# A small store of zeros early on ACT, and the last slab stored whole, in a FiLM layer kernel

## The chip, the cores and the metric

The kernel runs on one core of a Trainium2 chip. The metric is device time in microseconds (us) of one execution; lower is better. Executions of this kernel mostly agree within a few tenths of a microsecond. Some are longer: where one is over 1.5% above the fastest of the same kernel it is marked slow. A ratio is the mean time of one kernel's fast runs over the mean of the other's fast runs of the same rounds, so it is not quite the ratio of the medians that I quote.

## The reference

```python
batch, seq, dim, cond_dim = 32, 512, 256, 64          # all float32
gamma = conditioning @ gamma_proj                     # [32, 256]
beta  = conditioning @ beta_proj
return x * (1 + gamma[:, None, :]) + beta[:, None, :] # [32, 512, 256]
```

16.8 MB of x come in and 16.8 MB go out. Nothing else is large.

## The kernel before

x is cut into four slabs of eight batches. A slab is 128 partitions x 32 rows of 256 numbers, 4 MB. All four fit in SBUF at once, so no load ever waits for a buffer. SyncE issues the loads, ACT issues the small loads and all stores. DVE works on 11 rows of each group of 16 and GpSimd (POOL) on 5, and each group is stored when both are done.

```python
cond_s = consts.tile([batch, cond_dim], f32)
nc.scalar.dma_start(out=cond_s, in_=conditioning)
gbproj = consts.tile([cond_dim, 2 * dim], f32)
nc.scalar.dma_start(out=gbproj[:, :dim], in_=gamma_proj)
nc.scalar.dma_start(out=gbproj[:, dim:], in_=beta_proj)

for s in range(SLABS):                       # 5 loads: 8 + 24 rows, then 32, 32, 32
    ...
        nc.sync.dma_start(out=xs[:, r : r + n, :], in_=x_v[s, :, r : r + n, :])
# ... identity, matmuls: gamma and beta per partition in PSUM (gb_p) and SBUF (gb_s)
for s in range(SLABS):
    ...
    for r0 in range(0, ROWS, GROUP):         # two groups of 16 rows
        nc.vector.scalar_tensor_tensor(out=v, in0=rows(g_p, nv), scalar=1.0, in1=v, ...)
        nc.gpsimd.tensor_tensor(out=w, in0=w, in1=rows(g_s, nw), op=ALU.mult)
        nc.vector.tensor_add(out=v, in0=v, in1=rows(b_p, nv))
        nc.gpsimd.tensor_tensor(out=w, in0=w, in1=rows(b_s, nw), op=ALU.add)
        nc.scalar.dma_start(out=o_v[s, :, r0 : r0 + GROUP, :],
                            in_=xs[:, r0 : r0 + GROUP, :])
```

## Time and profile before

| | before |
|---|---|
| time, median of 6 runs | 84.43 us (84.36 to 84.56) |
| profiled span (length of the one run that the profile shows) | 82.6 us |
| DMA queues, share of 16 engines' time | 48.6% + 48.0% |
| DVE / POOL busy | 49.9 / 46.2 us |
| first load packet, last store packet | 1.74 us, 81.38 us |

Read it as one resource that never rests. Sixteen DMA engines serve two queues, q1 (loads, issued on SyncE) and q10 (all that ACT issues). A packet here is one row of a transfer on one engine: 8, 24 or 32 KB per partition for the loads, 16 KB for the stores, 1 KB for gamma and beta, 4 bytes for a semaphore, the counter by which a finished transfer releases what waits for it. Below, a queue's ring is the line of its packets that wait for one engine, and a turn is what an engine takes from one ring before it goes over to the other. DVE and POOL are busy for 60% and 56% of the span and idle at its end.

### The profile page before, as it was taken

The numbers are of one execution on the slowest core, as the hardware profiler recorded it, in microseconds if no ns is written. First come the engines' busy times: TensorE is split into PE (matmuls) and PEld (weight loads), VectorE is DVE, ScalarE is ACT, GpSimd is POOL, SyncE is SP. The second block draws the span as 40 slices with busy tenths as digits, with TensorE's granted clock in tenths as the row PEclk, the third lists the DMA queues.
The fourth block names the chain that finished last, engine by engine and source line by source line (L and its number), as shares of the span: only waits on it lengthen the run. The fifth ranks groups of instructions, "written<-read, shape, count | busy, mean of one in ns | idle before, by whom it ended". The sixth has DMA issues, their size and how long they took to land.

```text
span 82.6 us, 156 instructions
## 1 busy us (share of the span) xinstructions
PE 9.1 (11%) x10; PEld 2.8 (3%) x10; DVE 49.9 (60%) x18; ACT 3.9 (5%) x9; POOL 46.2 (56%) x22
## 2 busy tenths in 40 slices
PE   0080000899600000000000000000000000000000
PEld 0100000443000000000000000000000000000000
DVE  2011000059999999999999999999999920000000
ACT  0600000034400000000000000000000000000000
POOL 2000000069999999999999999999995000000000
DMA  3899999969969989998889979899999999999992
GB/s 56 337 508 397 389 397 524 460 302 508 508 270 492 508 381 381 413 476 381 381 381 556 460 302 460 381 468 421 429 452 389 468 421 421 460 389 452 437 421 87
DMA packets 2080, 33.69 MB, mean 408 GB/s; under 512 B 288, under 2 KB 416, under 8 KB 416
## 3 DMA queue, kind: packets, MB, share of 16 engines
q1 hardware_dynamic: 720, 16.78, 48.6%
q10 hardware_dynamic: 1360, 16.92, 48.0%
HBM read 16.92 MB, written 16.78 MB: 408 GB/s over the span
## 4 chain that ended last, share of the span: by engine, by line
DVE 49%; DMA 16%; issue 11%; PE 2%; ACTq 1%; ACT 1%
DVE xs L100 30%; DVE xs L103 19%; DMA gbproj<-in_beta_proj_dram 16%; PE gb_p L79 2%; ACTq L50 1%; ACTq L48 0%; ACT gb_s L82 0%; ACT gb_s L85 0%
## 5 line engine op out<-in xcount | busy, mean ns | idle before, releaser
L102 POOL TENSOR_TENSOR xs<-xs,gb_s 128x1280 f32<-128x1280 f32 x8 | 23.0, 2895 | 16.2 <-ACT gb_s L82 16.2
L100 DVE SCALAR_TENSOR_TENSOR xs<-gb_p,xs 128x2816 f32<-128x2816 f32 x8 | 24.7, 3083 | 10.9 <-ACT gb_s L85 10.9
L103 DVE TENSOR_TENSOR xs<-xs,gb_p 128x2816 f32<-128x2816 f32 x8 | 24.7, 3086 | 0.3
L104 POOL TENSOR_TENSOR xs<-xs,gb_s 128x1280 f32<-128x1280 f32 x8 | 23.0, 2893 | 0.0
L79 PE MATMUL gb_p<-gbproj,cond_T 64*128 64x512 f32 x8 | 7.2, 1074 | 8.9 <-DMA gbproj<-in_beta_proj_dram 8.9
L74 DVE COPY cond_T<-cond_T_p 64x512 f32<-64x512 f32 x1 | 0.7, 683 | 4.3 <-PE cond_T_p L72 4.3
L79 PEld LDWEIGHTS gb_p<-gbproj,cond_T 64*128 64x128 f32 x8 | 2.5, 328 | 13.7 <-issue 13.7
L72 PE MATMUL cond_T_p<-rident,cond_s 32*64 32x512 f32 x2 | 1.9, 1065 | 3.9 <-DMA cond_s<-in_conditioning_dram 3.9
L82 ACT ACTIVATE gb_s<-gb_p 128x256 f32<-128x256 f32 x4 | 1.5, 383 | 16.4 <-PE gb_p L79 16.4
L85 ACT COPY gb_s<-gb_p 128x256 f32<-128x256 f32 x4 | 1.5, 367 | 0.0
L82 ACT ACT_TABLE_LOAD x1 | 1.3, 1283 | 2.4 <-issue 2.4
L67 DVE COPY rident<-ident 32x512 f32<-32x512 f32 x1 | 0.4, 416 | 1.2 <-POOL ident masks.py:199 1.2
L72 PEld LDWEIGHTS cond_T_p<-rident,cond_s 32*64 32x64 f32 x2 | 0.3, 202 | 3.9 <-issue 3.9
masks.py:197 POOL MEMSET ident<- 32x32 f32 x1 | 0.1, 114 | 0.3 <-POOLq L121 0.3
masks.py:199 POOL TENSOR_SCALAR_AFFINE_SELECT ident<-ident 32x32 f32<-32x32 f32 x1 | 0.2, 202 | 0.1
L121 POOL MEMSET const-float32-0.0<- 128x1 f32 x1 | 0.1, 103 | 0.2 <-issue 0.2
L121 POOL MEMSET const-bfloat16-1.0<- 128x1 bf16 x1 | 0.1, 106 | 0.0
L121 POOL MEMSET const-uint8-127<- 128x1 uint8 x1 | 0.1, 106 | 0.0
L121 POOL MEMSET const-float32-1.0<- 128x1 f32 x1 | 0.1, 103 | 0.0
## 6 DMA issues: line engine op xcount, KB each, us to landing
out_dram<-xs ACTq DMA_DIRECT2D x8, 2048.0 KB, 18.2
xs<-in_x_dram SPq DMA_DIRECT2D x3, 4096.0 KB, 32.9
xs<-in_x_dram SPq DMA_DIRECT2D x1, 3072.0 KB, 12.2
xs<-in_x_dram SPq DMA_DIRECT2D x1, 1024.0 KB, 4.6
gbproj<-in_gamma_proj_dram ACTq DMA_DIRECT2D x1, 64.0 KB, 9.1
gbproj<-in_beta_proj_dram ACTq DMA_DIRECT2D x1, 64.0 KB, 12.9
cond_s<-in_conditioning_dram ACTq DMA_DIRECT2D x1, 8.0 KB, 3.0
```

The lines of the kernel that those rows point to most:

```text
L50: nc.scalar.dma_start(out=gbproj[:, :dim], in_=gamma_proj)
L67: nc.vector.tensor_copy(out=rident.rearrange("p (b g) -> p b g", g=REP), in_=ident.to_broadcast([batch, batch, REP]),)
L72: nc.tensor.matmul(cond_T_p, lhsT=cond_s, rhs=rident, start=True, stop=True)
L74: nc.vector.tensor_copy(out=cond_T, in_=cond_T_p)
L79: nc.tensor.matmul(p_t, lhsT=cond_T[:, s * P : (s + 1) * P], rhs=gbproj, start=True, stop=True)
L82: nc.scalar.activation(out=s_t[:, :dim], in_=p_t[:, :dim], func=mybir.ActivationFunctionType.Identity, bias=1.0, scale=1.0)
L85: nc.scalar.copy(out=s_t[:, dim:], in_=p_t[:, dim:])
L100: nc.vector.scalar_tensor_tensor(out=v, in0=rows(g_p, nv), scalar=1.0, in1=v, op0=ALU.add, op1=ALU.mult)
L102: nc.gpsimd.tensor_tensor(out=w, in0=w, in1=rows(g_s, nw), op=ALU.mult)
L103: nc.vector.tensor_add(out=v, in0=v, in1=rows(b_p, nv))
L104: nc.gpsimd.tensor_tensor(out=w, in0=w, in1=rows(b_s, nw), op=ALU.add)
L121: nc = _bacc.Bacc("TRN2", target_bir_lowering=False, num_devices=1)
```

## The change

A store of 16 rows of zeros (16 KB) into the output is added. The zeros are issued on ACT, ahead of gamma and beta; their place in the output is overwritten later by the first real store. The last slab goes out in one 4 MB store in place of two of 2 MB. The number of DMAs stays at sixteen. What the zeros were meant to achieve isn't stated; the form suggests an attempt to reorder what is in flight around the small loads and to save one DMA at the end.

```diff
     nc.scalar.dma_start(out=cond_s, in_=conditioning)
+
+    zero = consts.tile([16, dim], f32)
+    nc.gpsimd.memset(zero, 0.0)
+    nc.scalar.dma_start(out=o_v[0, 0:16, 0, :], in_=zero)
     gbproj = consts.tile([cond_dim, 2 * dim], f32)
...
+            last = s == SLABS - 1
...
-            nc.scalar.dma_start(out=o_v[s, :, r0 : r0 + GROUP, :],
-                                in_=xs[:, r0 : r0 + GROUP, :])
+            e0 = 0 if last else r0
+            if not last or r0 + GROUP == ROWS:
+                nc.scalar.dma_start(out=o_v[s, :, e0 : r0 + GROUP, :],
+                                    in_=xs[:, e0 : r0 + GROUP, :])
```

## The prediction

> **What bounds the kernel now.** I read the page's slices and queues first, then the chain of waits in order of time, then the stretches of the end, then the source line of the stores, and last the single packet records of the DMA engines in the trace.
>
> ```profile
> PE   0080000899600000000000000000000000000000
> DVE  2011000059999999999999999999999920000000
> POOL 2000000069999999999999999999995000000000
> DMA  3899999969969989998889979899999999999992
> q1 hardware_dynamic: 720, 16.78, 48.6%
> q10 hardware_dynamic: 1360, 16.92, 48.0%
> ```
>
> The DMA row is full from the second slice to the last but one, while DVE and POOL are idle for the last fifth. q1 holds the loads issued on SyncE, q10 everything issued on ACT. Together their packets fill 96.6% of the time of 16 engines: 0.966 x 82.57 us = 79.8 us by the page. I counted it from the packet records too: 128 load packets of 8 KB at 0.309 us, 128 of 24 KB at 0.92, 384 of 32 KB at 1.213, and 1024 store packets of 16 KB at 0.611. That is 39.5 + 118 + 466 + 626 = 1250 us, with the small packets about 1256, over 16 engines 78.5 us. The first load packet starts at 1.74 us and the last store packet ends at 81.38. So 78.5 of these 79.6 us is data, and the kernel is **bound by DMA bytes**, 16.8 MB in and 16.8 MB out, not by the DVE that leads the chain of waits:
>
> ```profile
> 1.72 12.90 DMA gbproj<-in_beta_proj_dram
> 14.76 2.06 PE gb_p L79 x2
> 17.52 3.10 DVE xs L100
> 63.49 3.09 DVE xs L103
> ```
>
> Columns: start, length, what. The reader is to see two things. Compute starts at 17.5 us, because the small beta load takes 12.9 us to land. And the chain's last compute ends at 63.49 + 3.09 = 66.58 us, 16 us before the end. Those 16 us are stores draining:
>
> ```profile
> 64.00:68.00 4.00, 0.00 (x0) 0.00 (x0) 2.58 (x1) 0.00 (x0) 0.00 (x0) 1.00 1.06 455
> 68.00:72.00 4.00, 0.00 (x0) 0.00 (x0) 0.00 (x0) 0.00 (x0) 0.00 (x0) 1.00 0.98 418
> 72.00:76.00 4.00, 0.00 (x0) 0.00 (x0) 0.00 (x0) 0.00 (x0) 0.00 (x0) 1.00 1.02 438
> 76.00:80.00 4.00, 0.00 (x0) 0.00 (x0) 0.00 (x0) 0.00 (x0) 0.00 (x0) 1.00 1.00 430
> ```
>
> These are stretches of the tail; the last two columns are the DMA share and GB/s. Nothing computes after 68 us and the DMA engines never rest. How far ahead the stores are issued is in the source line of the stores:
>
> ```profile
> L105 ACTq DMA_DIRECT2D out_dram<-xs x8: 338/339/368, 25.9 to 66.7; - x8
> DMA to landing us min/median/max: 15.1/18.2/22.6
> ```
>
> Even the quickest store takes 15.1 us to land, though its own 128 packets need only 8 x 0.61 = 4.9 us: the rest is queueing behind earlier stores. From the records, the two stores of the last slab are issued at 60.5 and 66.67 us, and their first packets start at 71.34 and 76.20. **This backlog is what the change eats into.**
>
> **What the Trainium skill says.** All four places are in its page "DMA: Bandwidth & Descriptors". (1) "Specifications" gives a fabric ceiling of 435 GB/s; the trace agrees, 16 x 16384 B in 0.611 us is 429 GB/s, so there is no rate to gain. (2) "Queues, rings and completion order" says that each engine round-robins between the queue rows it has work for, by packets, several descriptors each. The trace agrees with the alternation but at a finer grain: from 7.7 to 12.6 us an engine mostly takes one 24 KB x packet (0.92 us), then one 1 KB gbproj packet (0.046), in turn. (3) "Why a DMA increments its semaphore by 16 and not by 1" says that the rows of a copy are split over the largest count up to 16 that divides them; 16 partitions then give one 1 KB packet per engine. The trace agrees on a neighbour: the 32 rows of conditioning show two packets on each engine whose sequence I rebuilt. (4) "Two DMAs through the same engine are not ordered" says that a later DMA may not rely on the queue for order but must wait on the first one's semaphore. The first real store overwrites the zeros, so it may get such a wait; no run here shows it yet.
>
> **The change part by part.**
>
> Zeros, the memset. One more POOL instruction ahead of the identity. A 32x32 memset shows 0.114 us and a 1280-element POOL product 2.89 us; between these I estimate 0.2 to 0.5 us for 256 elements, at about 0.74 us. It makes rident later by as much, hidden, since conditioning lands only at 3.9 us.
>
> Zeros, the issue. ACT finishes issuing conditioning at 1.14 us, waits up to about 0.3 us for the memset, then spends some 0.45 us (its neighbours: 0.40 and 0.51) on the issue. Gamma and beta go out about 0.5 to 0.8 us later.
>
> Zeros, the transfer. Sixteen packets, one per engine: 0.046 us, and 0.009 for the semaphore packet. On the bounding resource that is **+0.055 us**.
>
> Zeros, the turns. What matters more is that gbproj now stands behind a data packet and a semaphore packet in the same ring, and each can cost one turn against an x packet. Two turns of 0.92 us are 1.8 us, and since the last beta packets then fall among the 32 KB packets of 1.21 us, up to 2.4. If the zeros slip in before 4.8 us, among the 8 KB packets of 0.31 us, little but the later issue remains. The next x load may also get its descriptors made ahead of gamma's. I take **compute start +2.4 us, range +0.5 to +3.6**. DVE then goes on without a gap as now, so its end moves from 66.6 to about 69.0 us.
>
> The last store whole. One store of 4096 KB at 69.0 instead of 60.5 and 66.7. Its packets will be 32 KB: 8 per engine at 1.213 (the loads' 32 KB figure) = 9.70 us, against the two stores' 2 x 4.86 = 9.72 now, from the spacing of their first packets. One semaphore packet less: **about -0.02 us**. When is it needed? The stores before it keep the engines busy until 71.4 us, a moment set by bytes and not by when each was issued. From issue to first packet an unloaded DMA took 1.0 us (first x load, 0.74 to 1.74) to 1.44 (conditioning, 0.74 to 2.18). So the whole store can start at about 69.0 + 1.4 = 70.4, still 1 us ahead of need. In general **the slack is 71.4 - 66.7 - 1.4 = 3.3 us minus the delay of compute**.
>
> Sum on the bounding resource: 0.055 - 0.02 = +0.03 us, and no new gap. The reads that the engines do while the first store is late are reads that they do not have to do afterwards, so a later start of stores costs nothing in itself. I put 84.5 us, a trifle over 84.44 for the chance of a gap.
>
> **The rivals.**
>
> *The tail runs dry.* If compute is delayed by 3.6 us, or if a store's packets come later after issue than 1.4 us, the engines idle before the last store. For it: the first real store, issued at 25.94, shows its first packet only at 29.76, 3.8 us later. Against: then 32 KB load packets were ahead of it in the engines, which at 68 us are gone. With 3.8 in place of 1.4 and a delay of 2.4 us, the gap is 66.7 + 2.4 + 3.8 - 71.4 = 1.5 us, time 86.0 (+1.8%). With a delay of 3.6 us it is 2.7, time 87.1 (+3.2%).
>
> *A load waits for a semaphore.* The DMA queue's own waits hold this line:
>
> ```profile
> SPq L59 <- DMA gbproj<-in_gamma_proj_dram: 7.6, 1, 7.6
> ```
>
> The fifth x load waits until gamma has landed, though it has no use for it; landing records show they share a semaphore. Sixteen DMAs run on eight such semaphores, and one more DMA at the front shifts who shares with whom. If a late load fell on a store's semaphore (first store landed: 44 us), reads could stop at about 35 us. Stores already queued would fill part, the time might be 86 to 90 us. Against: the count stays sixteen (one more, one less), and a shift by one gives the loads other early partners (conditioning, zeros, gamma, beta), all landed by 17 us, when x data for the engines is queued until 22 us and, with the fourth load, until 35.
>
> *Faster through larger packets or an early first write.* At the first store packet the two engines I rebuilt idle for 0.26 and 0.43 us after a load packet. If that is a cost of the first write to HBM that the zeros pay earlier, it only moves. Bytes per us are equal for 16 KB (26.8 GB/s an engine) and 32 KB (27.0). At most 0.4 us, time 84.0.
>
> **Range and chances.** The main line gives 84.4 to 84.6. The dry tail reaches a few tenths to 1.5 us in perhaps one case of eight and over 2% in about one of thirty; the semaphore case I hold under 2%; a gain over 2% (1.7 us) has no source, as 78.5 us of data remain. Range 84.1 to 85.6; faster 0.01, same 0.94, slower 0.05.
>
> **What would show it.** Right: beta lands at 16 to 17 us rather than 14.6; DVE starts at 18 to 21 us and ends 1 to 3.6 us later; DMA row full up to the last slice; the first packet of the whole store follows the last of the sixth without a gap; the tail's rate stays at 430 GB/s; first load packet to last store packet still about 79.6 us. Wrong: a slice with less DMA between 67 and 73 us (dry tail), reads that pause between 22 and 48 us (semaphore), or store packets whose bytes per us differ from the loads'.

## The result, and the profile after

The changed kernel takes 84.58 us in the median of six runs, two of which are slow (85.72 and 86.05). Its four fast runs are 84.36, 84.46, 84.54 and 84.61. The ratio of fast runs to those before is 1.0007, with a 95% interval of 0.9991 to 1.0022: the same time.

Inside, much moved. First, the slices and the queues of the kernel after:

```profile
PE   0090000049990000000000000000000000000000
DVE  2003000001999999999999999999999996000000
POOL 3000000002999999999999999999999800000000
DMA  2899999799799969999999899999999999999790
q1 hardware_dynamic: 720, 16.78, 48.4%
q10 hardware_dynamic: 1248, 16.93, 47.9%
```

The blocks of DVE and POOL have slid to the right by more than a slice (a slice is 2.06 us); the DMA row is as full as before. The bytes are the same but for the zeros, and there are fewer packets on q10 because the last ones are larger. (DMA shares above 1 in the stretches suggest that a packet is booked whole where it starts, so an uneven digit beside a large packet is no gap; the packet records show none here.)

Then four pieces of the chain that ended last, with start and length:

```profile
2.20 15.22 DMA gbproj<-in_beta_proj_dram
17.56 2.05 PE gb_p L83 x2
20.31 3.10 DVE xs L105
66.29 3.09 DVE xs L108
```

Beta was issued at 2.20 us instead of 1.72 and took 15.22 us to land instead of 12.90. So DVE starts its first slab at 20.31 us instead of 17.52, **2.79 us later**, and ends at 69.38 instead of 66.58, later by the same 2.8 us. All of DVE's work, the chain of half the span, is late by 2.8 us, and the kernel isn't.

The source line of the stores of the kernel after:

```profile
L112 ACTq DMA_DIRECT2D out_dram<-xs x7: 338/338/360, 28.7 to 69.5; - x7
DMA to landing us min/median/max: 12.3/17.4/19.9
```

The whole store is issued at 69.5 us. By the packet records its first packet starts at 71.34 us, the same moment as the first half's before, and its last one ends at 81.41 against 81.38. Two stretches of the tail (the last two columns are DMA share and GB/s):

```profile
68.00:72.00 4.00, 0.00 (x0) 0.00 (x0) 1.38 (x1) 0.00 (x0) 0.00 (x0) 1.00 1.08 463
76.00:80.00 4.00, 0.00 (x0) 0.00 (x0) 0.00 (x0) 0.00 (x0) 0.00 (x0) 1.00 1.14 492
```

DVE now works until 69.4 us, and the DMA share stays around 1. Last, the DMA queue's own waits after:

```profile
SPq L63 <- DMA gbproj<-in_gamma_proj_dram: 8.0, 1, 8.0
SPq L63 <- DMA cond_s<-in_conditioning_dram: 2.0, 1, 2.0
```

The last x load still waits for gamma, and an earlier one now waits 2.0 us for conditioning, a partner that it hadn't before. Both are over by 13 us, and the packet records show no engine idle for it.

### The profile page after: what moved, and what is told of

It reads as the page before. It is cut to its first block, busy times and chain, and to the rows that moved or that the text cites. A ratio compares the mean times of both kernels' runs of the same rounds, so it can differ in the third digit from the quotient of the medians.

```text
span 82.6 us, 156 instructions
## 1 busy us (share of the span) xinstructions
PE 9.1 (11%) x10; PEld 2.8 (3%) x10; DVE 49.9 (60%) x18; ACT 3.9 (5%) x9; POOL 46.5 (56%) x23
## 4 chain that ended last, share of the span: by engine, by line
DVE 49%; DMA 18%; issue 12%; PE 2%; ACTq 1%; ACT 1%; POOL 0%; POOLq 0%
DVE xs L105 30%; DVE xs L108 19%; DMA gbproj<-in_beta_proj_dram 18%; PE gb_p L83 2%; ACTq L54 1%; ACT gb_s L86 0%; ACT gb_s L89 0%; ACTq L52 0%; POOL ident masks.py:199 0%; POOL ident masks.py:197 0%; POOL zero L51 0%; POOLq L128 0%
```

## The experiments

**My theory** (A and A1 in the texts below): the kernel is bound by DMA bytes from 1.7 to 81.4 us; the zeros delay gamma and beta by taking turns in the ACT ring ahead of them; that delay is hidden because the stores already queued keep the engines busy until 71.3 us. **The rivals**: the two parts cancel (C: zeros cost, the whole store gains); stores are late by as much as compute, so that the backlog plays no part (B); and, for the delay, the write (A2) or the later issue (A3) counts rather than turns. The runs of one group share a chip and the runs of the kernel before.

### Each part alone: zero_only and whole_only

```diff
# zero_only: the change without the whole last store
-            e0 = 0 if last else r0
-            if not last or r0 + GROUP == ROWS: ...
+            nc.scalar.dma_start(out=o_v[s, :, r0 : r0 + GROUP, :], in_=xs[:, r0 : r0 + GROUP, :])
# whole_only: the change without the zeros
-    zero = consts.tile([16, dim], f32)
-    nc.gpsimd.memset(zero, 0.0)
-    nc.scalar.dma_start(out=o_v[0, 0:16, 0, :], in_=zero)
```

> The zeros alone, the last slab stored in halves as before. Theory A (the DMA engines are bound by bytes and a late compute start is hidden behind the stores already queued): 84.4 to 84.6 us, DVE starts near 20.3 us instead of 17.5, last packet still near 81.4. Rival C (the two parts cancel: the zeros cost time and the whole store gives it back): 85 us or more, since compute starts 2.8 us later.

> The whole last store alone, without zeros. Theory A: 84.4 us within 0.2, DVE starts at 17.5 us, the whole store is issued at 66.7 us and its first packet is at about 71.3, right behind the store before it. Rival C: under 84.0 us, since the whole store would be worth something by itself.

whole_only: 84.59 us in the median, one slow run of six, ratio of fast runs 1.0001 (0.998 to 1.0023). Compute starts as before, and the whole store's first packet follows the store before it at once. The whole store alone is worth nothing.

zero_only: of six runs three are marked slow, one (85.74) lies just below the mark and counts as fast, and two are 84.62 and 84.55. The ratio, 1.0053 (0.9998 to 1.0108), carries that 85.74. So this run says "same" with a wide interval, and is not clean proof by itself. The two low runs are within 0.02 us of what theory A said (84.4 to 84.6). zero_late3, below, has the zeros, the halves and a further delay on top, and gives a clean 84.6.

### Running the backlog out: after_late3, zero_late3, after_late1

An idle copy on DVE ahead of the first slab delays all later DVE work and adds no DMA byte. Its result is never read.

```diff
+    late = consts.tile([P, 11, dim], f32)                      # [P, 4, dim] in after_late1
+    nc.vector.tensor_copy(out=late, in_=rows(gb_p[0][:, :dim], 11))
     for s in range(SLABS):
         xs = slabs[s]
```

after_late3 adds it to the changed kernel, zero_late3 to the kernel with the zeros and the halves, and after_late1 a shorter one to the changed kernel.

> The changed kernel with one idle copy of 128x2816 (about 3 us) on DVE ahead of the first slab, to push the last issue from 69.5 to about 72.5 us; it adds no DMA byte. Theory A with the slack of the prediction (first packet 1.4 us after the issue, needed at 71.4): the first packet of the whole store comes at 73.9 us, a gap of 2.5 us in the DMA row, time 87.0 us. With a first packet 3.8 us after the issue (the other figure of the prediction): gap 4.9 us, 89.4 us; but then the changed kernel itself would have shown a gap. Rival B (the backlog plays no part, stores are simply late by as much as compute): 87.5 us and no gap that belongs to the whole store alone.

> The same idle copy, with the zeros, but the last slab stored in halves. Theory A: the first half is issued at about 66.3 us, ahead of the 71.3 us at which it is needed, the second at 72.5, ahead of 76.2: no gap, 84.4 to 84.7 us. Rival B: 87.5 us as with the whole store.

> The changed kernel with a shorter idle copy, 128x1024, about 1.1 us on DVE: the whole store is issued at about 70.6 us. In the run with the 3 us copy the first packet came 0.85 us after the issue. With that latency the first packet would be due at 71.45, against 71.34 needed: gap 0.1 us, time 84.5 to 84.8 us. With the 1.4 us of the prediction: gap 0.7 us, time 85.1 to 85.3.

after_late3: 85.89 us, all four runs fast, ratio 1.0169 (1.0144 to 1.0193). Here the store is late. The DMA row, the stores' source line, and stretches around the gap:

```profile
DMA  3898998997998898999888999999999998595990
```

```profile
L115 ACTq DMA_DIRECT2D out_dram<-xs x7: 338/339/361, 29.3 to 72.2; - x7
```

```profile
68.00:72.00 4.00, 0.00 (x0) 0.00 (x0) 3.97 (x2) 0.00 (x0) 0.00 (x0) 1.00 0.77 328
72.00:74.00 2.00, 0.00 (x0) 0.00 (x0) 0.13 (x1) 0.00 (x0) 0.00 (x0) 1.00 0.61 262
74.00:78.00 4.00, 0.00 (x0) 0.00 (x0) 0.00 (x0) 0.00 (x0) 0.00 (x0) 1.00 1.14 492
```

The share falls to 0.77 and 0.61 between 68 and 74 us. The whole store is issued at 72.2 us and its first packet starts at 73.05: **0.85 us from issue to first packet** with the queues empty. The engines finished the store before it between 71.2 and 71.6 us; in the packet records an engine idles 1.7 us on average there, and 1.44 us on the engine that ran dry last. The time grew by 1.4 us. (The whole interval lies above 1.) I had expected 87.0: the issue came 0.3 us earlier than I had put it, the first packet 0.55 us sooner after the issue, and the end moved by about the shortest of the gaps (last packet at 82.90 us instead of 81.41).

zero_late3: 84.63 us, one slow run of four, ratio 1.0007 (0.9982 to 1.0033). The same delay, the same zeros, but a first half that could be issued earlier. Its stretches at the same place:

```profile
68.00:72.00 4.00, 0.00 (x0) 0.00 (x0) 3.96 (x2) 0.00 (x0) 0.00 (x0) 1.00 1.00 430
72.00:74.00 2.00, 0.00 (x0) 0.00 (x0) 0.18 (x1) 0.00 (x0) 0.00 (x0) 1.00 1.01 434
```

Full speed. DVE ends at 72.2 us here too. This pair shows that a late compute end is free as long as a store is queued, and that the whole store is what takes the queue away.

after_late1: 84.52 us, one slow run of four, ratio 0.9998 (0.997 to 1.0026). The whole store is issued at 70.5 us and follows the store before it without a gap, its first packet at 71.57. With 0.85 us from issue to first packet, 70.5 is about the last moment that still fits, and the time agrees.

### Where the 2.8 us come from: zero_behind, issue_only, issue_later

zero_behind issues the zeros behind beta. issue_only has no zeros, but lets a memset of gbproj hold the gamma load back; issue_later has two such memsets. All three store the last slab whole.

```diff
# zero_behind
-    (the three lines of zero)
     gbproj = consts.tile([cond_dim, 2 * dim], f32)
     nc.scalar.dma_start(out=gbproj[:, :dim], in_=gamma_proj)
     nc.scalar.dma_start(out=gbproj[:, dim:], in_=beta_proj)
+    (the three lines of zero)
# issue_only, issue_later
-    (the three lines of zero)
     gbproj = consts.tile([cond_dim, 2 * dim], f32)
+    nc.gpsimd.memset(gbproj, 0.0)          # twice in issue_later
```

> The changed kernel with the store of zeros issued behind gamma and beta instead of ahead of them; same bytes, same packets. Theory A1 (the 2.8 us by which compute starts later are turns in the ACT ring that the zeros and their semaphore take ahead of gbproj): DVE starts at 17.5 us as in the kernel before, within 0.3. Rival A2 (the extra write slows the loads or the engines by itself, wherever it stands): DVE starts near 20. Time 84.4 to 84.6 us with both, since the delay is hidden.

> No zeros; in their place a GpSimd memset of the gbproj tile that the gamma load has to wait for, so that gamma and beta are issued 0.3 to 0.6 us later without any packet ahead of them. Last slab whole. Theory A1 (turns): DVE starts at 17.5 to 18.5 us. Rival A3 (the later issue is what counts, because the descriptors of a large x load then go first): DVE starts near 20.3 us. Time 84.4 to 84.6 us with both.

> As the run with one memset of gbproj, which moved the gamma issue only from 1.17 to 1.29 us, but with two of them, so that gamma goes out at about 1.8 us, as late as or later than the 1.65 us of the changed kernel, and still with no packet of zeros ahead of it. Theory A1 (turns taken by the zeros): DVE starts between 17.9 and 18.9 us. Rival A3 (the later issue lets the descriptors of the next x load go first): DVE starts near 20.3 us. Time 84.4 to 84.6 us with both.

From the timelines of zero_behind and of issue_later, the issue of gamma and DVE's first work on the slabs (start, length, what):

```profile
1.17 0.51 ACTq L51 DMA_DIRECT2D gbproj<-in_gamma_proj_dram  x1
17.67 3.09 DVE L105 SCALAR_TENSOR_TENSOR xs<-gb_p,xs 128x2816 f32<-128x2816 f32 x1 [10.93 <-ACT gb_s L89]
```

```profile
1.87 0.53 ACTq L53 DMA_DIRECT2D gbproj<-in_gamma_proj_dram  x1
18.91 3.09 DVE L104 SCALAR_TENSOR_TENSOR xs<-gb_p,xs 128x2816 f32<-128x2816 f32 x1 [12.13 <-ACT gb_s L88]
```

zero_behind (84.72 us, four fast runs, ratio 1.0019, 0.9989 to 1.0049): gamma goes out at 1.17 us as before and DVE starts at 17.67, 0.15 us after the kernel before. The write by itself costs at most that 0.15 us; its place costs the rest.

issue_later: gamma goes out at 1.87 us, 0.70 later than before and later than the 1.65 of the changed kernel, and DVE starts at 18.91, 1.39 us late, half of 2.79. That falsifies the rival that lateness of issue is all (20.3), though 18.91 is at the very edge of what I had put down for turns. The packet records say where the 1.39 come from: beta lands at 14.5 to 14.9 us on seven engines and at 15.7 to 16.0 on nine, one 32 KB packet later, and compute waits for the last. Gamma's first packet is at 5.73 to 6.16 us on the seven, but only from 6.55 us on on the nine: they had their first turn without it. So lateness of issue can itself lose a turn. Its time isn't settled: of its two runs one is 84.53 and the other 85.72, both counted fast.

issue_only was a weak test: its memset moved gamma by only 0.12 us, to 1.29. DVE starts at 17.88 us; gamma's first packet lies between 5.73 and 6.12 us on all sixteen engines, so no turn is lost. Ratio of fast runs 1.001 (0.9986 to 1.0033).

Engine by engine, the changed kernel shows the turns. On the engine that I rebuilt from the packet records, before the change the first gamma packet is at 5.75 us and the last beta packet at 12.62. After it, the zeros' packet is at 5.94 us, its semaphore packet at 6.89, the first gamma packet at 7.81 and the last beta packet at 15.35: 2.06 us late at gamma, 2.73 at beta, with an x packet of 0.91 us after each of the zeros' two packets. All sixteen engines agree. Before, gamma's first packet is at 5.61 to 5.93 us. After, the zeros' packet has that turn (5.68 to 6.20), the zeros' semaphore packet the next (6.63 to 7.15) and gamma's first packet the one after (7.54 to 8.06), with no turn lost between, and so it is in all five other profiles with the zeros in front. Beta's last semaphore packet moves from 14.16 to 16.97 us, by 2.81. So the two turns account for the whole delay, and the 0.48 us of later issue shows no cost of its own, since gamma's turn came only at 7.54. What that lateness would cost without the zeros lies between two runs: none at 1.29 us (issue_only), a turn on nine engines at 1.87 (issue_later).

### The floor: no_compute

```diff
-            nc.vector.scalar_tensor_tensor(...)
-            nc.gpsimd.tensor_tensor(...)
-            nc.vector.tensor_add(...)
-            nc.gpsimd.tensor_tensor(...)
             nc.scalar.dma_start(out=o_v[s, :, r0 : r0 + GROUP, :], in_=xs[:, r0 : r0 + GROUP, :])
```

> Wrong result on purpose: the kernel before without the DVE and GpSimd work of the slabs, so that each store may go as soon as its x data has landed; it measures what the DMA traffic alone takes. Theory A (bound by DMA bytes from 1.7 to 81.4 us): 84.0 to 84.5 us although every store is issued much earlier. Rival B (the late start of compute, 17.5 us, is what bounds the kernel): well under 80 us.

The result is wrong on purpose. 84.46 us, four fast runs, ratio to the kernel before 0.9996 (0.9977 to 1.0015).

```profile
DVE  2003000000000000000000000000000000000000
DMA  3899999899698999998899988999999999999992
```

Without any slab work, with the first store issued at 22.6 us instead of 25.9, the kernel takes the same time. All 50 us of DVE and 46 us of POOL are hidden behind DMA. This is the strongest single piece of evidence that the DMA traffic alone sets the time.

### The halves' own limit: halves_late

Three idle copies of 3.1 us in zero_late3's place of one.

```diff
+    nc.vector.tensor_copy(out=late, in_=rows(gb_p[0][:, :dim], 11))   # three times
```

> Zeros, the last slab in halves, and three idle copies of 128x2816 on DVE (9.3 us), to run the slack of the halves out. Theory A: DVE ends at about 66.6 + 2.7 + 9.3 = 78.6 us; the last half has its first packet 0.85 us after its issue, at 79.4, and its data takes 4.86 us more plus about 0.3 us of spread over the engines: last packet at 84.5 us instead of 81.4, time 87.5 us, +3.1. With the whole store the same delay would end 4.9 us later still. Rival B (backlog plays no part): 84.5 + 2.7 + 9.3 = 96 us or more.

87.5 us, four fast runs, ratio 1.0344 (1.0325 to 1.0362): the number was hit, but not by the step that I gave. With so much delay the scheduler ordered DVE's work otherwise (two products, then two sums), so the sixth store was issued only at 69.0 us, and there the engines ran dry: its first packet is at 69.87, again 0.85 us after the issue. They had run dry once before, for about 1 us at 56.8 us: the fourth store was issued at 57.01 and its first packet is at 57.86, the same 0.85. The last three stores then follow each other without a gap, 69.87 + 3 x 4.86 = 84.45, and the records have the last packet end at 84.62. So the run confirms the latency and that the backlog sets the time, but its 87.5 is partly a coincidence of two ways to nearly the same moment, and the limit of the last half itself was not reached: it was issued at 78.13 us and its first packet follows the seventh store at 79.62 without a gap.

### The slow state

The two profiles (zero_only, issue_only) look alike: the 32 KB load packets take 1.36 us instead of 1.213 from about 14 us until the stores begin (30 to 33 us), and the stores take 0.611 us as ever. One stretch, zero_only's and then that of the kernel before (DVE and POOL do one instruction fewer in zero_only because compute starts later there; the last column, GB/s, is the point):

```profile
14.00:28.00 14.00, 7.16 (x8) 2.47 (x8) 7.36 (x3) 2.59 (x8) 7.61 (x3) 1.00 1.05 407
```

```profile
14.00:28.00 14.00, 7.16 (x8) 2.50 (x8) 10.41 (x4) 2.59 (x8) 10.70 (x4) 1.00 1.00 433
```

The kernel before had one slow run too (86.17, of 31 runs in all), and so had whole_only and issue_only, without zeros. It was more frequent in some variants (two of six in the changed kernel, three of six in zero_only), but the counts are small, and I have no cause. Whether the change makes it likelier is left open.

## Why the prediction was right

Predicted 84.5 us, range 84.1 to 85.6, "same" at 0.94; measured 84.58. Point by point:

- **Bound by DMA bytes**: right, and no_compute shows it (84.46 us without the slab work). One number of that step was loose: I counted 78.5 us of data from common packet durations. Summing each packet's own duration gives 79.8 us before and 79.6 after, because some load packets take longer (32 KB: 1.237 us on average, 1.213 in the middle). The difference that I left between data and the busy stretch is mostly slower packets, not idle engines.
- **The memset and the issue**: the memset took 0.30 us (estimated 0.2 to 0.5), gamma and beta went out 0.48 us later (said 0.5 to 0.8, so a little less).
- **The turns**: said +2.4 us on compute start, range 0.5 to 3.6; measured +2.79. Mechanism shown by zero_behind, where the same packets behind beta cost 0.15 us. The zeros did not slip in among the 8 KB packets: their first packet is at 5.68 us. The two turns are in the records of every engine. They cost more than 2.4 mainly because the 32 KB packets among which beta then falls took 1.28 to 1.36 us there, not 1.21; two of them are 2.6 us or more. The later issue cost nothing on top, though issue_later shows that it can cost a turn by itself (1.39 us for 0.70).
- **The whole store**: said -0.02 us; whole_only shows ratio 1.0001, and its packets take 1.213 us as said.
- **The slack**: the mis-sized term. I took 1.4 us from issue to first packet and so a slack of 3.3 us. after_late3 and halves_late measure 0.85 us, so the slack is 71.34 - 66.67 - 0.85 = 3.8 us. The change uses 2.8 of it. after_late1, at 3.8 us of delay, is still free; after_late3, at 5.5, costs 1.4.
- **The rivals**: the dry tail is real but wasn't reached; after_late3 reaches it. Its second version, 3.8 us from issue to first packet, belongs to a store behind large load packets: no_compute's first store has it again (22.57 to 26.36 us), empty queues don't. The semaphore shift happened as foreseen, with a harmless partner. If the first real store waits for the zeros, that is free: they have landed by 7.5 us and it is issued at 28.7. No gain came from an early first write or from larger packets. One reading of mine was wrong: the 0.26 and 0.43 us at the first store are not idle time. No engine has a gap there; the load packets just ahead of the first store are longer, 1.21 to 1.66 us, and in the changed kernel still 1.21 to 1.60, so the early zeros did not take that away.

## What to carry to other kernels

Before you judge a change, ask which resource is full to the end and how far ahead of need its work is queued: 2.8 us of delay on the chain that the profile follows back were free here, because the stores queued ahead left 3.8 us of slack. Merging the last stores saved nothing and cut that slack, since a merged store can be issued only when its last part is done. With the halves it would have been 76.20 - 66.67 - 0.85 = 8.7 us for the last one (my estimate from these runs; no run isolates it). A tiny DMA ahead of a small load that others wait for cost two whole turns of the other queue's packets here (2.8 us); behind it, 0.15 us. Put it behind.

## What the Trainium skill lacked or had wrong

- "DMA: Bandwidth & Descriptors", "Queues, rings and completion order", has an engine drain a packet of some 9 to 17 descriptors from one ring before it switches. The trace shows rows, not descriptors, and here an engine switched after single rows: one 24 KB x row (0.92 us), then one 1 KB gbproj row (0.046 us). No place there says that the 4-byte semaphore packet takes a turn too; in the changed kernel the zeros' semaphore packet (6.89 us) stands between two x packets of 0.91 us.
- The same page, "Latency and other measured facts", gives about 600 ns to the first byte of such a DMA. From the start of the issue to the first packet the runs show 0.85 us with empty queues (72.2 to 73.05, and 69.02 to 69.87); the issue itself takes 0.34 us of that, so it is 0.51 from its end, and the page does not say from where it counts. They show 3.8 us for a store behind 32 KB load packets (25.94 to 29.76, and 22.57 to 26.36), a case that it doesn't list.
- The same page, "Where 436 GB/s comes from", has the HBM side bind at about 358 GB/s for HBM to SBUF transfers. The sentence lacks its condition: the page's own table of single loads has up to 425, and the note under it says that these are for one core alone and that 358 holds with both cores of a pair streaming. The runs agree with the note: on this one core the stores moved 429 GB/s (16 packets of 16 KB in 0.611 us), and the whole span, start and end included, 408 GB/s.
